# The adaLN weight tiles of a hybrid RWKV-7 and pooling layer: 128 x 512 of one K tile, or four K tiles by 128 columns

## The chip, the cores and the metric

The kernel runs on one NeuronCore of one Trainium2 chip. The metric is device time of one execution, in microseconds (us).

## The reference

One layer of width 2048 (`D`) for 1024 latent tokens and 256 context tokens, in fp32. Only the part that the change touches, and what uses it, matters here:

```
silu_c, silu_cc = silu(c), silu(c_ctx)                   # two vectors of 2048
mod_lat = silu_c @ w_ada + b_ada                         # w_ada: 2048 x 6144
mod_ctx = silu_cc @ w_ada + b_ada
sh, sc, gt = split(mod, 3)                               # shift, scale, gate; 2048 each
h  = rms_norm(x, norm_g) * (1 + sc) + sh                 # latent and context tokens
p  = h @ w_in                                            # 2048 x 6400, combined projection
y  = rwkv7 scan and pooling heads of p, gated
x  = x + gt * (y @ w_out);  return rms_norm(x, final_g)
```

The product of two vectors with `w_ada` reads 50 MB of weights for very little arithmetic.

## The kernel before

Names: PE is TensorE, DVE VectorE, ACT ScalarE, POOL GpSimd, SP SyncE, whose queue issues most DMAs in program order. The kernel is written against a tile framework. Its pools give a tile one of a tag's `bufs` buffers, and a DMA into a buffer waits for the readers of the tile that had it before. The framework orders the instructions of each engine by its own estimate before anything runs; on the chip each engine then goes through its list in that order.

`w_ada` is cut into 12 column blocks `w` of 512 columns (shift 0 to 3, scale 4 to 7, gate 8 to 11) and 16 K tiles `kt` of 128 rows. A weight tile before the change is one K tile by one block, 128 x 512 fp32, 256 KB. The activations `silu` are the stationary operand: 32 columns, of which two are in use (latent and context). The weight tile is the moving operand. `mod_row` (lines 177 to 179) sends K tile `kt` to column group `kt % 4`, that is to PSUM partitions 32 g to 32 g + 31, so that a block gathers four partial sums in four groups of rows. Line 224 (or line 506 for the gate) then multiplies the copied rows with `sel`, which adds the four groups.

The program has four stages in a row:

- Modulation (to about 240 us). `xs`, the tokens, are loaded and squared; `mod(4)` with its tiles in the buffers of `hhi` and `hlo` comes first. Then `mod(5)`, `mod(6)`, `mod(7)`, `mod(0)` to `mod(3)` follow. Beside each stands one `quarter` of two projection tiles: fp16 matmuls of lines 152 to 154, three for each product (`whi` with `hhi`, `whi` with `hlo`, `wlo` with `hhi`), 72 in a quarter, 48 of 512 columns and 24 of 256. `scaled(q)` and `moved(q)` on DVE and ACT make the next `hhi` and `hlo` from the modulation just computed. I call the stretch from one `mod`'s first tiles to the next one's a period. Weight tiles `wa` have a ring of `WAB` = 4 buffers.
- Preparation (to about 970 us): for each of eight j three projection tiles on PE, and beside them the scan's preparation (`prep_kk`, line 379; `prep_scan`, lines 430 and 431 with ACT's tanh, line 437). For j below 4, `gate_row(j)` is issued too, with weight tiles `wg` in a ring of `FB` = 2 buffers.
- The scan with its filler of projections, and the output projection with the residual. Neither reads `w_ada`.

The tiles' DMA and matmul, before:

```
            for kt in range(KT):
                wt = room[kt].bitcast(F32) if room else wap.tile([128, 512], F32, tag="wa", bufs=WAB, name=nm("wa"))
                dma(wt, I["w_ada"][w, kt // 4, :, kt % 4])
                mod_row(kt, wt, ps)
```

Of the kernel before, what the change touches and what calls it, by code (L numbers as in the profile page):

```python
# [7 lines left out]
F32 = mybir.dt.float32  # L8
# [11 lines left out]
KT = 16  # L20
# [25 lines left out]
FB = 2  # L46

WAB = 4
# [10 lines left out]
def hybrid_layer_kernel(ctx: ExitStack, tc: tile.TileContext, I, out, dbg=None):  # L59
    nc = tc.nc  # L60
    mm = nc.tensor.matmul
    V, S, G = nc.vector, nc.scalar, nc.gpsimd
    dma = nc.sync.dma_start
# [8 lines left out]
    def nm(s):  # L72
        cnt[0] += 1
        return f"{s}_{cnt[0]}"

    def bank(tag, bufs=1):
        return psum.tile([128, 512], F32, tag=tag, bufs=bufs, name=nm("ps"))
# [25 lines left out]
    def make_silu(pool):  # L103
        silu = pool.tile([128, KT, 32], F32, name=nm("silu"))
        th0 = pool.tile([128, KT, 2], F32, name=nm("th0"))
        V.memset(silu, 0.0)
        S.activation(th0, cv, AF.Tanh, scale=0.5)
        V.tensor_scalar(th0, th0, 1.0, 0.5, op0=ALU.add, op1=ALU.mult)
        V.tensor_tensor(silu[:, :, 0:2], cv, th0, ALU.mult)
        return silu  # L110
# [18 lines left out]
    wp = ctx.enter_context(tc.tile_pool(name="wp", bufs=1))  # L129
# [44 lines left out]
    idma(sel, I["sel"])  # L174
    silu = make_silu(hc_pool)

    def mod_row(kt, wt, ps):
        g = kt % 4
        mm(ps[32 * g:32 * g + 32, :], silu[:, kt, :], wt, start=(kt < 4), stop=(kt >= 12))


    with ExitStack() as p0:
        xp = p0.enter_context(tc.tile_pool(name="xp", bufs=1))
        wap = p0.enter_context(tc.tile_pool(name="wap", bufs=3))
# [18 lines left out]
        shp = xp.tile([128, KT, 2], F32, name="shp")  # L203
# [10 lines left out]

        def mod(w, room=None):
            ps = bank(("B1", "XU")[w % 2])
            for kt in range(KT):
                wt = room[kt].bitcast(F32) if room else wap.tile([128, 512], F32, tag="wa", bufs=WAB, name=nm("wa"))
                dma(wt, I["w_ada"][w, kt // 4, :, kt % 4])
                mod_row(kt, wt, ps)  # L220
            rows = wp.tile([128, 512], F32, tag="f", bufs=FB, name=nm("rows"))
            S.copy(rows, ps)
            for i in range(4):
                mm(ps[:, 2 * i:2 * i + 2], rows[:, 128 * i:128 * i + 128], sel[:, 0:2], start=True, stop=True)
            V.tensor_tensor(
                modc[:, 4 * w:4 * w + 4, :], ps[:, 0:8].rearrange("p (a b) -> p a b", b=2),
                par[:, PC_BADA + 4 * w:PC_BADA + 4 * w + 4].unsqueeze(2).broadcast_to([128, 4, 2]), ALU.add)
# [15 lines left out]
        def moved(q):  # L243
            V.tensor_scalar(shp[:, 4 * q:4 * q + 4, :], modc[:, 4 * q:4 * q + 4, :], HS, None, op0=ALU.mult)
            for kt, which, xv, rv, hi, lo in segments(q):
                sh = shp[:, kt, which:which + 1]
                S.activation(hi, xv, AF.Identity, bias=sh)
                V.scalar_tensor_tensor(lo, xv, sh, hi, op0=ALU.add, op1=ALU.subtract)

        mod(4, hhi[0:8] + hlo[0:8])  # L250
        for i, (o, n) in enumerate(chunks):
            ps = banks[0][i]
# [6 lines left out]
        for q in range(1, 4):  # L259
            mod(4 + q)  # L260
            quarter(ws, q - 1)
            ws = weights((24, 25), q)
            scaled(q)
        mod(0)
        quarter(ws, 3)
        ws = weights((8, 16), 0)
# [14 lines left out]
        for k in range(2):  # L281
            ps = bank(("B1", "XU")[k])
            for kq in range(4):
                wt = wap.tile([128, 512], F32, tag="wa", bufs=WAB, name=nm("we"))
                dma(wt.rearrange("p (k c) -> p k c", k=4), I["w_in"][24 + k, :, 4 * kq:4 * kq + 4, :])
                for g in range(4):
                    mm(ps[:, 0:2], wt[:, 128 * g:128 * g + 128], shp[:, 4 * kq + g, :],
                       start=(kq + g == 0), stop=(kq + g == 6))
            V.tensor_scalar(eb[:, k, :], ps[:, 0:2], 1.0 / HS, None, op0=ALU.mult)
        quarter(ws, 3)  # L290
# [205 lines left out]

    def gate_row(q):
        ps = bank("B1")
        for kt in range(KT):
            wt = wp.tile([128, 512], F32, tag="f", bufs=FB, name=nm("wg"))  # L500
            dma(wt, I["w_ada"][8 + q, kt // 4, :, kt % 4])
            mod_row(kt, wt, ps)
        rows = wp.tile([128, 512], F32, tag="f", bufs=FB, name=nm("rows"))
        S.copy(rows, ps)
        ps = bank("B1")
        mm(ps[0:32, :], sel[:, 2:34], rows, start=True, stop=True)
        gt = wp.tile([1, 512], F32, tag="f", bufs=FB, name=nm("gt"))
        bg = wp.tile([1, 512], F32, tag="f", bufs=FB, name=nm("bg"))
        dma(bg, I["b_gt"][0:1, 512 * q:512 * q + 512])
        V.tensor_tensor(gt, ps[0:1, :], bg, ALU.add)  # L510
        dma(sGT[0:1, 512 * q:512 * q + 512], gt)
# [18 lines left out]
    for j in range(NP):  # L530
        held = {}
        pre = banks if j == 0 else (None, None)
        kx = hc_pool.tile([128, NALL + 4], F32, tag="k", bufs=2, name=nm("k"))[:, 0:NALL]
        beside(shifted(8 + j, kx, pss=pre[0]))
        drain()
        vx = p1.tile([128, NALL], F32, tag="v", name=nm("v"))
        side.append(prep_kk(j, kx, held))
        beside(shifted(16 + j, vx, pss=pre[1]))
        side.append(prep_v(j, vx))
        rx = p1.tile([128, NTOK], F32, tag="r", name=nm("r"))  # L540
        beside(shifted(j, rx, with_ctx=False, tags=("XU", "B1") if j == 0 else ("d0", "d1")))
        side.append(prep_scan(j, kx, vx, rx, held))
        if j < 4:
            gate_row(j)
# [4 lines left out]
    with ExitStack() as p2s:  # L549
# [368 lines left out]
        for bi, (Q, g) in enumerate(batches):  # L918
            if g == 0:
                carry = {}  # L920
            for s in range(4):
                k = 4 * bi + s
# [121 lines left out]
def layout(x, c, ctx, c_ctx, norm_g, w_ada, b_ada, w_in, shift_mu, w0, w_up, a0, a_up,  # L1044
           k_k, k_a, r_k, lnx_g, lnx_b, w_pool, pool_scale, w_out, final_g):
    import numpy as np

    def cols(a, n):
        return np.asarray(a).reshape(n, 128).T

    L = {}
    L["xT"] = np.asarray(x)[0].T.reshape(KT, 128, NTOK)
    L["ctxT"] = np.asarray(ctx)[0].T.reshape(KT, 128, NCTX)
    L["x"] = np.asarray(x)[0]
    L["cvec"] = np.stack([cols(c, KT), cols(c_ctx, KT)], axis=2)
    L["w_ada"] = np.asarray(w_ada)[0].reshape(4, 4, 128, 12, 512).transpose(3, 0, 2, 1, 4)
    L["w_in"] = np.asarray(w_in)[0].reshape(KT, 128, 50, 128).transpose(2, 1, 0, 3)
    L["w_out"] = np.asarray(w_out)[0].reshape(KT, 128, 4, 512).transpose(2, 0, 1, 3)
    L["w_pool"] = np.asarray(w_pool)[0].reshape(4, 2, 128, 256).transpose(2, 0, 1, 3)
    L["w_up"] = np.asarray(w_up)[0]  # L1060
    L["a_up"] = np.asarray(a_up)[0]
    L["b_gt"] = np.asarray(b_ada)[:, 4096:6144]
    L["final_g"] = np.asarray(final_g)
    L["par"] = np.concatenate([
        cols(norm_g, 16), cols(np.asarray(shift_mu)[0, 0], 26), cols(np.asarray(shift_mu)[0, 1], 26),
        cols(w0, 16), cols(a0, 16), cols(k_k, 8), cols(k_a, 8), cols(r_k, 8), cols(lnx_g, 8), cols(lnx_b, 8),
        cols(pool_scale, 8), cols(b_ada, 48)], axis=1)
    f = np.float32
    L["ident"] = np.eye(128, dtype=f)
    bo = np.zeros((128, 128), f)  # L1070
    bo[:64, :64] = 1
    bo[64:, 64:] = 1
    ex = np.zeros((128, 128), f)
    hs = np.zeros((128, 32), f)
    for h in range(2):
        ex[h::32, 64 * h:64 * h + 64] = 1
        hs[64 * h:64 * h + 64, h] = 1
    L["heads"] = np.concatenate([bo, ex, hs], axis=1)
    r, t = np.arange(128), np.arange(64)[None, :]
    m = np.zeros((128, 2, 2, 128), f)  # L1080
    for h in range(2):
        for d in range(2):
            u = np.where((r // 64 != h) & (d == 1), 63 - r % 64, r % 64)[:, None]
            m[:, h, d, :64] = u < t
            m[:, h, d, 64:] = u <= (63 - t if d else t)
    L["mask"] = m
    rcv = np.zeros((128, 4, 64), f)
    pos = np.arange(64)
    for g, w in enumerate(WINDOWS):
        n = np.clip(pos + w // 2 - 1, 0, 63) - np.clip(pos - w // 2, 0, 63) + 1  # L1090
        rcv[:, g] = (1.0 / n.astype(f)).astype(f)
    L["rc"] = rcv
    se = np.zeros((128, 130), f)
    se[0::32, 0] = 1
    se[1::32, 1] = 1
    se[0::32, 2:] = 1
    L["sel"] = se
    return L
# [18 lines left out]
```

## Time and profile before

| | |
|---|---|
| time, median of 3 runs | 2450.76 us (2447.87 to 2464.92) |
| the profiled execution | 2454.08 us, with a span of 2452.3 us on the engines |
| mean granted TensorE clock | 0.986 |
| busy | PE 2327.6 us (95%), DVE 1639.5 (67%), ACT 786.3 (32%), POOL 389.0 (16%) |
| line 179, `wa` tiles | 224 records (two for each fp32 matmul), 50.8 to 233.5 us |
| line 179, `wg` tiles | 128 records, 286.6 to 620.0 us |
| DMA of `w_ada` | 192 x 256 KB |

A row of the view in order of time gives start in us, length in us, engine, line, operation and `output<-inputs`, with partitions x columns and a count of merged records. The recorded length of a matmul includes its way through the array, so successive rows overlap: what a matmul costs PE is the distance between starts, not the length. A row of the view of stretches gives busy us and, in brackets, the number of instructions of each engine; at its end stand the granted clock, the busy share of the DMA engines and GB/s.

### The profile page before, as it was taken

To read this page: it belongs to the slowest core of one execution; us is meant where nothing else is said; L and a number is where in the kernel's file an instruction comes from. 1 tells how busy PE (TensorE), PEld (TensorE's weight loads), DVE (VectorE), ACT (ScalarE), POOL (GpSimd) and SP (SyncE) were. 2 spreads that over 40 slices of the span, in tenths; PEclk is the share of its full clock that TensorE was granted. 3 is DMA by queue.
4 is the path that set the end of the run, shared out by engine and by line. 5 is a ranking of instruction groups with operands and counts; after the bars stand their busy time and mean duration, and the time that the engine had idled before them with its cause. 6 is when DMAs were issued, how large, how long until landed. Compare 5 with 4: busy or idle time off the path is not lost. (4 is left out here: it accounts for less than half of the span.)

```text
span 2452.3 us, 48416 instructions
## 1 busy us (share of the span) xinstructions
PE 2327.6 (95%) x18702; PEld 1334.8 (54%) x18702; DVE 1639.5 (67%) x3432; ACT 786.3 (32%) x1307; POOL 389.0 (16%) x682
## 2 busy tenths in 40 slices
PE   3999999999999999989998999999999999999997
PEld 0333443534444544445666566656665555788886
DVE  7533664563765666488787977989889784444446
ACT  5233533333444445111122212321232122333334
POOL 3000000100000000113333233333333321000000
PEclk9999999999999999999898999999999999999999
DMA  8666364555543543666556455665565542745546
GB/s 301 183 191 181 100 154 124 141 142 134 131 101 101 126 116 103 177 175 151 149 148 167 131 149 160 164 174 148 158 181 162 141 114 78 236 130 169 183 134 202
DMA packets 421589, 374.45 MB, mean 153 GB/s; under 512 B 232984, under 2 KB 298552, under 8 KB 421104
## 3 DMA queue, kind: packets, MB, share of 16 engines
q1 hardware_dynamic: 403824, 331.75, 48.9%
q0 software_dynamic: 17536, 39.61, 5.7%
q8 instruction: 148, 2.42, 0.4%
q14 instruction: 81, 0.66, 0.1%
HBM read 286.53 MB, written 83.37 MB: 151 GB/s over the span
## 5 line engine op out<-in xcount | busy, mean ns | idle before, releaser
L152 PE MATMUL ps<-hhi,whi 128*128 128x512 f16 x1600 | 611.0, 383 | 2.6 <-ACT whi L144 1.9
L153 PE MATMUL ps<-hlo,whi 128*128 128x512 f16 x1600 | 611.4, 383 | 0.3
L154 PE MATMUL ps<-hhi,wlo 128*128 128x512 f16 x1600 | 610.9, 383 | 0.1
L152 PEld LDWEIGHTS <-whi 128*128 128x128 f16 x1888 | 185.2, 98 | 210.9 <-issue 54.5
L154 PEld LDWEIGHTS <-wlo 128*128 128x128 f16 x1888 | 185.5, 98 | 194.0 <-issue 34.2
L153 PEld LDWEIGHTS <-whi 128*128 128x128 f16 x1888 | 185.7, 98 | 186.7 <-issue 35.3
L145 DVE SCALAR_TENSOR_TENSOR wlo<-wraw,whi 128x512 f16<-128x512 f32 x200 | 136.0, 683 | 131.9 <-ACT whi L144 131.2
L144 ACT ACTIVATE whi<-wraw 128x512 f16<-128x512 f32 x200 | 124.2, 629 | 308.3 <-PE ps L153 198.6
L696 DVE TENSOR_TENSOR tm<-TT 64x30 f32<-64x30 f32 (+2 forms) x600 | 195.5, 326 | 18.0 <-DMA TT<-dn 9.1
L698 DVE TENSOR_TENSOR TT<-TT,tm 64x30 f32<-64x30 f32 (+2 forms) x600 | 197.7, 330 | 8.5
L975 PE MATMUL ps<-wolo,mhi 128*128 128x512 f32 x512 | 199.7, 390 | 2.2 <-DVE wolo L971 2.1
L975 PE MATMUL ps<-wohi,mlo 128*128 128x512 f32 x512 | 198.9, 389 | 0.0
L975 PE MATMUL ps<-wohi,mhi 128*128 128x512 f32 x512 | 198.2, 390 | 0.4 <-ACT wohi L970 0.4
L971 DVE TENSOR_TENSOR wolo<-wo,wohi 128x512 fp32r<-128x512 f32 x144 | 97.9, 689 | 147.1 <-ACT wohi L970 146.8
L970 ACT CAST wohi<-wo 128x512 fp32r<-128x512 f32 x144 | 89.2, 621 | 176.9 <-PE ps L975 151.4
L664 PE MATMUL ps<-AR,BK 64*128 64x128 f32 (+1 forms) x1280 | 122.6, 296 | 17.8 <-DMA BK<-sBK 8.7
L664 PEld LDWEIGHTS ps<-AR,BK 64*128 64x128 f32 x1280 | 105.4, 198 | 46.2 <-issue 13.4
L744 POOL DMA_DIRECT2D SUV<-sV x160 | 96.6, 607 | 128.5 <-PE ps L805 65.1
L975 PEld LDWEIGHTS ps<-wolo,mhi 128*128 128x128 f32 x512 | 96.1, 188 | 24.0 <-DVE wolo L971 4.1
L975 PEld LDWEIGHTS ps<-wohi,mhi 128*128 128x128 f32 x512 | 95.9, 188 | 21.8 <-ACT wohi L970 2.0
L975 PEld LDWEIGHTS ps<-wohi,mlo 128*128 128x128 f32 x512 | 96.1, 188 | 19.7
L813 POOL TENSOR_TENSOR S<-St,PCt 128x256 f32<-128x256 f32 x76 | 57.5, 757 | 262.5 <-DVE St L807 231.1
(226 smaller groups left out, 3450.8 us busy)
## 6 DMA issues: line engine op xcount, KB each, us to landing
wraw<-in_w_in SPq DMA_DIRECT2D x200, 256.0 KB
BK<-sBK SPq DMA_DIRECT2D x156, 256.0 KB
wo<-in_w_out SPq DMA_DIRECT2D x144, 256.0 KB
wa<-in_w_ada SPq DMA_DIRECT2D x112, 256.0 KB
wg<-in_w_ada SPq DMA_DIRECT2D x64, 256.0 KB
AR<-sAR SPq DMA_DIRECT2D x64, 256.0 KB
sBK<-BK SPq DMA_DIRECT2D x32, 320.0 KB
sBK<-BK SPq DMA_DIRECT2D x16, 640.0 KB
```

The source lines that it names most:

```text
L144: S.activation(whi, raw, AF.Copy, scale=WS)
L145: V.scalar_tensor_tensor(wlo, raw, WS, whi, op0=ALU.mult, op1=ALU.subtract)
L152: mm(ps[:, :n], w[0][:, k, :], hi[kt][:, o:o + n], start=(kt == 0), stop=False)
L153: mm(ps[:, :n], w[0][:, k, :], lo[kt][:, o:o + n], start=False, stop=False)
L154: mm(ps[:, :n], w[1][:, k, :], hi[kt][:, o:o + n], start=False, stop=(kt == KT - 1))
L664: mm(ps[h][:, 64 * ns * u:64 * ns * (u + 1)], BK[hs, p, d, :], AR[hs, :, p, d, :], start=True, stop=True)
L696: V.tensor_tensor(tm, TT[:, 0:s, s:s + 1].broadcast_to([64, s, n]), TT[:, s:s + 1, s + 1:32].broadcast_to([64, s, n]), ALU.mult)
L698: V.tensor_tensor(TT[:, 0:s, s + 1:32], TT[:, 0:s, s + 1:32], tm, ALU.add)
L744: (idma if d else dma)(SUV[hss[1 - h], h, :, d, :], sV[Q, cn, h])
L970: S.copy(whi, raw)
L971: V.tensor_tensor(wlo, raw, whi.bitcast(F32), ALU.subtract)
L975: mm(banks[q, t], mix[k][m][:, tk], w, start=(k == order[0] and n == 0), stop=(k == order[-1] and n == 2))
```

## The change

A weight tile is now four K tiles by 128 columns: `[128, 4, 128]`, again 2 KB for each of 128 partitions. The host lays `w_ada` out so that a tile is one piece of memory. Tile `i` of a block holds column piece `c = i // 4` and K tiles `4 a` to `4 a + 3` with `a = i % 4`. Its four matmuls, of 128 columns each, go to the four column groups; before, one matmul of 512 columns went to one group. Number and size of DMAs, the sums, the buffers and everything behind the rows in PSUM stay. The last lines of the diff's middle part (`we`) only rename a shape.

```
-    def mod_row(kt, wt, ps):
-        g = kt % 4
-        mm(ps[32 * g:32 * g + 32, :], silu[:, kt, :], wt, start=(kt < 4), stop=(kt >= 12))
+    def mod_block(i, wt, ps):
+        c, a = i // 4, i % 4
+        for g in range(4):
+            mm(ps[32 * g:32 * g + 32, 128 * c:128 * c + 128], silu[:, 4 * a + g, :], wt[:, g],
+               start=(a == 0), stop=(a == 3))
...
-            for kt in range(KT):
-                wt = room[kt].bitcast(F32) if room else wap.tile([128, 512], F32, tag="wa", bufs=WAB, name=nm("wa"))
-                dma(wt, I["w_ada"][w, kt // 4, :, kt % 4])
-                mod_row(kt, wt, ps)
+            for i in range(16):
+                if room:
+                    wt = room[i].bitcast(F32).rearrange("p (g n) -> p g n", g=4)
+                else:
+                    wt = wap.tile([128, 4, 128], F32, tag="wa", bufs=WAB, name=nm("wa"))
+                dma(wt, I["w_ada"][w, i])
+                mod_block(i, wt, ps)
...
-                wt = wap.tile([128, 512], F32, tag="wa", bufs=WAB, name=nm("we"))
-                dma(wt.rearrange("p (k c) -> p k c", k=4), I["w_in"][24 + k, :, 4 * kq:4 * kq + 4, :])
+                wt = wap.tile([128, 4, 128], F32, tag="wa", bufs=WAB, name=nm("we"))
+                dma(wt, I["w_in"][24 + k, :, 4 * kq:4 * kq + 4, :])
...
-        for kt in range(KT):
-            wt = wp.tile([128, 512], F32, tag="f", bufs=FB, name=nm("wg"))
-            dma(wt, I["w_ada"][8 + q, kt // 4, :, kt % 4])
-            mod_row(kt, wt, ps)
+        for i in range(16):
+            wt = wp.tile([128, 4, 128], F32, tag="f", bufs=FB, name=nm("wg"))
+            dma(wt, I["w_ada"][8 + q, i])
+            mod_block(i, wt, ps)
...
-    L["w_ada"] = np.asarray(w_ada)[0].reshape(4, 4, 128, 12, 512).transpose(3, 0, 2, 1, 4)
+    L["w_ada"] = np.asarray(w_ada)[0].reshape(4, 4, 128, 12, 4, 128).transpose(3, 4, 0, 2, 1, 5).reshape(12, 16, 128, 4, 128)
```

The line of the adaLN matmul is 179 before and 181 after. The order of PE's list, too, comes out differently. In the modulation stage, in the period of `mod(6)`, PE's list before reads (names are tiles with their running number; `32x512` is 32 rows out by 512 columns):

```order
L179 MATMUL ps_594<-wa_619,silu_179 32x512
L179 MATMUL ps_594<-wa_622,silu_179 32x512
L154 LDWEIGHTS wlo_560
L154 MATMUL ps_334<-hhi_112,wlo_560 128x512
L152 LDWEIGHTS whi_559
L152 MATMUL ps_334<-hhi_113,whi_559 128x512
L153 LDWEIGHTS whi_559
L153 MATMUL ps_334<-hlo_129,whi_559 128x512
L179 MATMUL ps_594<-wa_625,silu_179 32x512
```

After the change, a stretch of the same period, where `x4` counts the matmuls of one tile:

```order
L181 MATMUL ps_690<-wa_721,silu_179 32x128 x4
L152 LDWEIGHTS whi_655
L152 MATMUL ps_334<-hhi_112,whi_655 128x512
L154 LDWEIGHTS wlo_656
L154 MATMUL ps_334<-hhi_111,wlo_656 128x512
L181 MATMUL ps_690<-wa_727,silu_179 32x128 x4
L152 LDWEIGHTS whi_655
L152 MATMUL ps_335<-hhi_112,whi_655 128x512
L152 LDWEIGHTS whi_655
L152 MATMUL ps_336<-chi_145,whi_655 128x256
```

Where one or two tiles stood between groups of three or more fp16 matmuls, one tile now stands between groups of two or three. A period still begins with four tiles in a row.

In the preparation stage, beside `prep_scan` of j = 1, PE's list before and then after reads:

```order
L153 MATMUL ps_2790<-hlo_125,whi_2794 128x512
L179 MATMUL ps_2726<-wg_2763,silu_179 32x512
L179 MATMUL ps_2726<-wg_2766,silu_179 32x512
L154 LDWEIGHTS wlo_2795
L154 MATMUL ps_2790<-hhi_109,wlo_2795 128x512
L152 LDWEIGHTS whi_2812
L152 MATMUL ps_2790<-hhi_110,whi_2812 128x512
```

```order
L437 MATMUL ps_3326<-lora_2080,ulo_3318 128x512
L181 MATMUL ps_3158<-wg_3207,silu_179 32x128 x4
L154 LDWEIGHTS wlo_3337
L154 MATMUL ps_3269<-hhi_116,wlo_3337 128x512
L152 LDWEIGHTS whi_3336
L152 MATMUL ps_3269<-hhi_117,whi_3336 128x512
L181 MATMUL ps_3158<-wg_3213,silu_179 32x128 x4
L436 LDWEIGHTS uhi_3317
L436 MATMUL ps_3330<-lora_2080,uhi_3317 128x512
```

A pair of gate tiles that stood together is now parted by two fp16 matmuls.

More of the change, by code (lines that the diff above doesn't have):

```diff
@@ L283, in hybrid_layer_kernel @@
             for kq in range(4):
-                wt = wap.tile([128, 512], F32, tag="wa", bufs=WAB, name=nm("we"))
-                dma(wt.rearrange("p (k c) -> p k c", k=4), I["w_in"][24 + k, :, 4 * kq:4 * kq + 4, :])
+                wt = wap.tile([128, 4, 128], F32, tag="wa", bufs=WAB, name=nm("we"))
+                dma(wt, I["w_in"][24 + k, :, 4 * kq:4 * kq + 4, :])
                 for g in range(4):
-                    mm(ps[:, 0:2], wt[:, 128 * g:128 * g + 128], shp[:, 4 * kq + g, :],
+                    mm(ps[:, 0:2], wt[:, g], shp[:, 4 * kq + g, :],
                        start=(kq + g == 0), stop=(kq + g == 6))
```

## The prediction

> **What bounds the kernel now.** I read the page first, then the stretches of the program, then single instructions in order of time.
>
> ```profile
> span 2452.3 us, 48416 instructions
> PE 2327.6 (95%) x18702; PEld 1334.8 (54%) x18702; DVE 1639.5 (67%) x3432; ACT 786.3 (32%) x1307; POOL 389.0 (16%) x682
> PE   3999999999999999989998999999999999999997
> PEclk9999999999999999999898999999999999999999
> ```
>
> PE is busy in every slice after the first, at full clock. So PE's time is what a change has to shorten, and it has to do so where PE itself is late and not where it waits. The adaLN matmuls stand in slices 1 to 11 only (40 to 620 us). The next view cuts the modulation stage into one period per `mod`, first for all instructions, then for line 179 (`mod_row`) alone.
>
> ```profile
> core 0: us, PE busy (x) PEld busy (x) DVE busy (x) ACT busy (x) POOL busy (x), PEclk, DMA share, GB/s
> 106.59:133.12 26.53, 26.01 (x113) 8.57 (x113) 14.38 (x23) 7.62 (x13) 0.00 (x0) 1.00 0.65 189
> 185.79:212.38 26.59, 25.95 (x114) 8.57 (x113) 8.18 (x13) 7.59 (x12) 0.16 (x3) 1.00 0.61 178
> ...
> 106.59:133.12 26.53, 11.53 (x32) 1.54 (x33) 1.00 0.65 189
> ```
>
> A period is 26.5 us, 11.5 of them line 179, while DVE, ACT and the DMA engines (0.65 of their time) have room. What line 179 costs PE is read from its neighbours (start, length, instruction):
>
> ```profile
> 59.31 0.38 PE L154 MATMUL ps<-hhi,wlo 128*128 128x512 f16 x1
> 59.52 0.38 PE L152 MATMUL ps<-hhi,whi 128*128 128x512 f16 x1
> 59.83 1.04 PE L179 MATMUL ps<-wa,silu 128*32 128x512 f32 x2
> 60.81 0.39 PE L153 MATMUL ps<-hlo,whi 128*128 128x512 f16 x1
> ...
> 106.38 0.27 PE L154 MATMUL ps<-chi,wlo 128*128 128x256 f16 x1
> 106.59 1.07 PE L179 MATMUL ps<-wa,silu 128*32 128x512 f32 x8
> 107.58 0.60 PE L152 MATMUL ps<-hhi,whi 128*128 128x512 f16 x2
> ```
>
> A plain fp16 matmul of 512 columns follows the one before after 0.21 us (59.31 to 59.52), one of 256 after half of it. One adaLN matmul (two records: fp32 goes in two passes) puts 59.52 to 60.81 = 1.29 us where 0.22 stood: it costs 1.07. Four of them, on four column groups, put 106.38 to 107.58 = 1.20 where 0.11 stood: 1.09. So a **run** of one to four matmuls of kernel before costs the same 1.07 us: the groups do work at once, but most runs use one or two. Counted in the order of PE, the 176 matmuls that stand between others (7 `mod` and 4 gates) make 120 runs: 71 in `mod`, 49 in the gates. 120 x 1.07 = 128 us.
>
> **What a run costs after the change.** No run of before has 128 columns on four groups. The nearest row is `prep_kk`'s line 379: also fp32, also 32 weight columns on each of four groups, other moving data for each, 320 columns.
>
> ```profile
> 272.07 0.38 PE L154 MATMUL ps<-hhi,wlo 128*128 128x512 f16 x1
> 272.38 0.75 PE L379 MATMUL ps<-sqk,heads 128*32 128x320 f32 x8
> 273.06 0.39 PE L152 MATMUL ps<-hhi,whi 128*128 128x512 f16 x1
> ```
>
> 0.99 us where 0.22 stood: 0.775. From 512 columns (1.09) to 320 (0.775) that is 1.64 ns a column, so 128 columns give 0.775 - 192 x 1.64 ns = **0.46 us** (my estimate; two passes of 0.105 and 0.25 for entering, leaving and the second pass's weights). A tile that directly follows a tile adds its two passes only. A weight load takes 108 ns, no less than a pass of 128 columns, so I put 0.22:
>
> ```profile
> L179 PEld LDWEIGHTS ps<-wa,silu 128*32 128x32 f32 x224 | 10.9, 108 | 34.2 <-issue 21.7 <-DMA wa<-in_w_ada 11.7 <-PE ps L153 0.8
> ```
>
> The tiles now make 151 runs: 92 of the 112 in `mod` (after four back to back, each tile stands alone) and 59 of the 64 in the gates. `mod`: 92 x 0.46 + 20 x 0.22 = 46.7 against 71 x 1.07 = 76.0, a gain of 29.3. Gates: 59 x 0.46 + 5 x 0.22 = 28.2 against 49 x 1.07 = 52.4, a gain of 24.2. **PE is given back 53.5 us.** `mod(4)`, the first, has 4, 2 and 10 tiles in a row in both orders and its groups are full already; I count it at 0.
>
> **What comes late next.** Its tiles. SP's queue waits for PE to free a buffer, and then PE for the landing:
>
> ```profile
> SPq L219 <- PE ps L179: 104.1, 69, 5.5
> ...
>   issue: 41.2, 103
>   DMA wg<-in_w_ada: 17.9, 23
>   DMA wa<-in_w_ada: 13.4, 20
> ...
> 107.66 0.33 SPq L219 DMA_DIRECT2D wa<-in_w_ada  x1
> ...
> 110.24 0.38 PE L154 MATMUL ps<-hhi,wlo 128*128 128x512 f16 x1
> 110.77 2.19 PE L179 MATMUL ps<-wa,silu 128*32 128x512 f32 x4
> 112.89 0.39 PE L153 MATMUL ps<-hlo,whi 128*128 128x512 f16 x1
> ```
>
> The four tiles at 106.59 give their buffers back together; SP issues the next from 107.66. PE takes the first at 110.77, 3.1 us after its issue and 0.2 later than PE was ready (entering takes 0.31), and can have the second at 112.89 - 0.98 = 111.9 only: 1.36 us of waiting in the period. Bounds for a tile's way from issue to use: 3.1 and about 4.2; I take 3.5, since the later tiles of a period are issued singly. With the run (0.36) and the way to SP (0.1) a buffer comes round in 4.0 us; four buffers (`WAB`) give a tile each 1.0 us. The new order asks for one each 0.95: behind the four tiles and 1.73 us of fp16 work, eleven gaps hold 5.4 us of fp16 work, 0.49 each, plus 0.46. So 11 x 0.05 = 0.6 us of new waiting in a period: 7 x 0.6 = **4 us back**. What stands behind the waiting matmul is all of PE's queue.
>
> The gates have two buffers (`FB`), so a tile each 4.0 / 2 = 2.0 us. Waits of 17.9 us for 4 gates show it already; one of them:
>
> ```profile
> 501.44 0.38 PE L431 MATMUL ps<-lora,ulo 128*128 128x512 f16 x1
> 501.75 2.23 PE L179 MATMUL ps<-wg,silu 128*32 128x512 f32 x4
> 503.91 0.39 PE L430 MATMUL ps<-lora,uhi 128*128 128x512 f16 x1
> ```
>
> A pair that should leave after 0.98 us leaves after 2.16. In the new order of the second gate 13.0 us of dense fp16 work, 2.2 us of lines 430 and 431 and twelve runs of 0.46 stand behind its first four tiles: 1.72 us for each of 12 tiles, less than two buffers give, and unevenly (every second gap is 0.2 to 0.6 us). That is 12 x 0.28 = 3.4 us of waiting from the mean alone and about as much from unevenness, against 17.9 / 4 = 4.5 before. Bounds: 0 and 5 us more per gate; I take 2, **8 us back**.
>
> The DMAs keep 2 KB for each partition (128 rows of 512 floats, now four pieces of 128 columns that lie side by side), so their time stays. SP's, DVE's and ACT's instructions are the same apart from places exchanged in these stages; from shortly behind the last gate to the end every engine's order is as before, so the two later stages only start earlier. DVE's 14.38 us of work in a period still fit into 23. The cover is thin in the first period alone, where the first `scaled` has to keep pace with PE; a rival below prices that.
>
> **Sum** against the profiled execution (2454.1, with a span of 2452.3): 2454.1 - 53.5 + 4 + 8 = 2412.6. The median of the runs, 2450.8, lies 3.3 lower: **2410** (2409.3 rounded up).
>
> **Rivals.**
>
> *Waits do not grow* (0.20). If a single tile comes in 3.1 us, four buffers give one each 0.9 and neither ring binds: 2454.1 - 53.5 = 2400.6, and up to 5 less if the waits after the four tiles fall, so 2392 to 2397 by the median. For it: the 3.1. Against: the 1.1 us that the second tile lagged.
>
> *The rings bind* (0.17). With 4.2 us from issue to use a buffer takes 4.66: 1.17 a tile in `mod`, 0.22 x 11 = 2.4 a period, 17 in all; 2.33 in the gates, 12 x 0.61 = 7.3 and 2 for unevenness against 4.5, 5 each and 20 in all: 2454.1 - 53.5 + 37 = 2437.6, or 2434 by the median; where half the tiles take so long, 2422. Then SP waits less for PE, and PE for the landing.
>
> *Other engines come late* (0.13). Where no gate stands beside the scan's preparation, PE waits for ACT's tanh:
>
> ```profile
> PE ps L430 <- ACT th L437: 8.6, 4, 2.8
> ```
>
> That is 2.2 us for each of the last four j, and nearly nothing while gates fill the gap. If it comes back in the four gate j, 9 us, and 3 in the first period: 2412.6 + 12, or 2421 by the median.
>
> *The second pass's loads are not hidden* (0.04). A load of 108 ns behind each first pass makes a run 0.57: 151 x 0.11 = 17 more, 2426. The row of the eight loads of line 379 speaks against it:
>
> ```profile
> 272.38 0.16 PEld L379 LDWEIGHTS ps<-sqk,heads 128*32 128x32 f32 x8 [0.42 <-issue]
> ```
>
> All eight lie in the first 0.16 us, beside matmuls whose first pass lasts 0.29. The Trainium skill, "TensorE: Matmul & The Clock Gate", section "Part 3: Packing small matmuls", says that weight loads overlap matmuls in flight only where the row group differs. Here all four share the rows, so by that rule this rival would hold; the trace does not agree.
>
> *The four run one after another* (0.03), the case that ends slower. If at 128 columns the groups did not overlap, a tile is 8 passes of 0.107 and 0.25 around them, 1.1 us: 151 x 1.1 + 25 x 0.86 = 188 against 128, +59, 2513. It turns to a loss once a run costs over (128 - 25 x 0.22) / 151 = 0.81 us. Against it: the 1.07 us that four of 512 columns take here.
>
> **How the numbers follow.** Forecast 0.43, rivals 0.20, 0.17, 0.13, 0.04 and 0.03. A measurement of this kernel tells about 1% (24.5 us, 2426) from no change. Faster by over 1%: 0.43 + 0.20 + 0.13 + half of 0.17 and of 0.04 = 0.86; within: 0.11; slower: 0.03. Range: from the waits that shrink (2392, and one for rounding) to past the loads' case (2426) and into the rings that bind (2422 to 2434): 2391 to 2430; beyond it lie a third of the rings' chance and the slower case.
>
> **What would show it.** In the profile after: line 181's tiles alone should stand 0.67 to 0.69 us from the fp16 matmul before to the one behind (now 1.29); a `mod` period 23.0 us (now 26.5: 10 x 1.07 less 13 x 0.46 and 3 x 0.22, and 0.6 of waiting); the gate stretch about 4 us shorter each; waits of line 181 for `wa` up by some 4 us and for `wg` by some 8; the time from the last gate to the end as before, 1830 us. The forecast is wrong if a run is not near 0.46, or if waits for tiles eat more than 25 us.

## The result, and the profile after

The kernel after takes 2387.79 us (median of 4 runs, 2384.81 to 2398.54) against 2449.32 for the kernel before (4 runs beside it): a ratio of 0.9746, 95% interval 0.9711 to 0.978. A later set with more runs gives 0.9764 (0.9735 to 0.9794). It is faster, as forecast, but by more: 61.5 us in the first comparison where 41 were forecast, and 2387.8 lies 3 us under the range. All 15 runs of it in this study together have a median of 2391.6 us.

The head of the page, after:

```profile
span 2387.4 us, 50718 instructions
PE 2252.8 (94%) x19854; PEld 1342.6 (56%) x19854; DVE 1637.4 (69%) x3432; ACT 785.7 (33%) x1307; POOL 380.2 (16%) x682
```

PE has 1152 instructions more (each tile eight records for two) and 75 us less to do. It still bounds the kernel: it is busy in 94% of a shorter span.

In the view of stretches, one period of the modulation, first all instructions, then line 181 alone:

```profile
98.15:119.66 21.51, 20.80 (x209) 9.48 (x209) 13.88 (x21) 7.13 (x12) 0.00 (x0) 1.00 0.69 221
141.38:164.50 23.12, 20.83 (x209) 9.49 (x208) 8.17 (x14) 8.71 (x16) 0.00 (x0) 1.00 0.65 206
...
98.15:119.66 21.51, 6.19 (x128) 2.70 (x129) 1.00 0.69 221
```

The period fell from 26.5 to between 21.5 and 23.1 us (forecast 23.0; the five periods after the first, from 75.40 to 186.75 us, have a mean of 22.3), and line 181 takes 6.19 of it where line 179 took 11.53. Instruction by instruction, a tile alone and four in a row:

```profile
122.55 0.38 PE L153 MATMUL ps<-hlo,whi 128*128 128x512 f16 x1
122.86 0.42 PE L181 MATMUL ps<-wa,silu 128*32 128x128 f32 x8
123.22 0.39 PE L154 MATMUL ps<-hhi,wlo 128*128 128x512 f16 x1
...
119.46 0.27 PE L154 MATMUL ps<-chi,wlo 128*128 128x256 f16 x1
119.66 1.08 PE L181 MATMUL ps<-wa,silu 128*32 128x128 f32 x32
120.67 0.39 PE L152 MATMUL ps<-hhi,whi 128*128 128x512 f16 x1
```

From the fp16 matmul before to the one behind it is 123.22 - 122.55 = 0.67 us where 1.29 stood, so a run costs 0.67 - 0.21 = 0.46: exactly the estimate. Four in a row cost 120.67 - 119.46 - 0.11 = 1.10, or 0.22 for each further tile (0.46 + 3 x 0.22 = 1.12).

The stages, worked out from the starts of the same instructions in four profiles of each kernel (first sum of `mod(4)`, last sum of `mod(3)`, first matmul of `prep_kk` for each j, first and last matmul of the scan's step, end), in us:

| stage | before (4 profiles) | after (4 profiles) | forecast change |
|---|---|---|---|
| modulation, to `prep_kk` of j = 0 | 272.4, 269.6, 270.2, 272.2 | 243.3, 243.7, 253.5, 243.8 | -25.3 |
| j = 0 to 4, with the four gates | 391.2, 389.3, 390.7, 389.4 | 366.6, 366.2, 365.4, 366.5 | -16.2 |
| j = 4 to 7 | 261.8, 261.6, 262.1, 261.6 | 261.2, 262.1, 262.4, 261.2 | 0 |
| to the first step of the scan | 171.0, 173.2, 171.4, 168.7 | 171.5, 172.2, 171.5, 171.4 | 0 |
| scan | 947.9, 944.3, 937.7, 942.2 | 936.9, 938.9, 933.4, 937.3 | 0 |
| to the end | 408.0, 408.5, 408.2, 409.8 | 407.9, 408.0, 409.3, 407.9 | 0 |

So three terms are to be explained: the modulation (27.5 without the one profile of 253.5), the gates (24.0 where 16.2 were forecast), and the scan, whose list of instructions did not change and which was 11.0 us shorter in the first pair of profiles.

### The profile page after: what moved, and what is told of

It reads as the page before. It is cut to its first block, busy times and chain, and to the rows that moved or that the text cites. A ratio compares the mean times of both kernels' runs of the same rounds, so it can differ in the third digit from the quotient of the medians.

```text
span 2387.4 us, 50718 instructions
## 1 busy us (share of the span) xinstructions
PE 2252.8 (94%) x19854; PEld 1342.6 (56%) x19854; DVE 1637.4 (69%) x3432; ACT 785.7 (33%) x1307; POOL 380.2 (16%) x682
## 5 line engine op out<-in xcount | busy, mean ns | idle before, releaser
L144 ACT ACTIVATE whi<-wraw 128x512 f16<-128x512 f32 x200 | 123.1, 628 | 262.4 <-PE ps L153 196.3
L670 PEld LDWEIGHTS ps<-AR,BK 64*128 64x128 f32 x1280 | 104.5, 196 | 44.7 <-issue 14.6
```

Of the source, the lines that this page charges most:

```text
L144: S.activation(whi, raw, AF.Copy, scale=WS)
L670: mm(ps[h][:, 64 * ns * u:64 * ns * (u + 1)], BK[hs, p, d, :], AR[hs, :, p, d, :], start=True, stop=True)
```

## Experiments

**The two kernels again, and each half of the change alone.** The first two are unchanged. Each half takes its part of `w_ada` in its own layout. The number behind "Measured" is the time as a share of the kernel before's, with its 95% interval.

Kernel before again: 

> The kernel before, unchanged, as a second profile. Theory A (the scan stage is 11.0 us shorter in the profile after only because one execution differs from another): its scan stage, from the first to the last matmul of line 781, falls anywhere between 936 and 948 us. Theory B (the change shortens it, although no instruction there stands in another place): again 947 to 949 us. Both: ratio 1.00, modulation and gates as in the first profile within 1 us (first tile behind the first period to the last gate tile 540 us).

Measured: 0.9999 (0.998 to 1.0018); scan stage 944.3 us. The modulation takes 2.8 us less than in the first profile and the gates 1.9 less, more than the 1 us that was expected; in the modulation the clock stood at half for 6.8 us there and for nothing here.

Kernel after again: 

> The kernel after, unchanged, as a second profile. Theory A: scan stage anywhere between 936 and 948 us. Theory B: 936 to 938 us again. Both: 54 us less than before up to the end of the preparation stage, ratio 0.975.

Measured: 0.9781 (0.9762 to 0.9801); scan stage 938.9 us; modulation and gates as in its first profile within 0.5 us.

New tiles in `mod` only:

```
...
-        for i in range(16):
-            wt = wp.tile([128, 4, 128], F32, tag="f", bufs=FB, name=nm("wg"))
-            dma(wt, I["w_ada"][8 + q, i])
-            mod_block(i, wt, ps)
+        for kt in range(KT):
+            wt = wp.tile([128, 512], F32, tag="f", bufs=FB, name=nm("wg"))
+            dma(wt, I["w_adb"][q, kt // 4, :, kt % 4])
+            mod_row(kt, wt, ps)
...
```

> New tiles in the eight mod blocks, old tiles in the four gates. If the stages add up: 29 us less by the first matmul of line 379, nothing from the gates, so 29 us in all (ratio 0.988), plus what the scan stage does. Theory A: no part of the scan's 11 us belongs to it more than to any other run. Theory B: the scan stage is shorter here or in the next kernel by some 5 to 11 us. A rival that the gates' gain is only work moved from the modulation (tiles and matmuls shifted across the border): the gates would take 2 us more or less than in the kernel before.

Measured: 0.9882 (0.9859 to 0.9904), 29.6 us. The gates take 388.6 us, 1.6 less than the mean of the kernel before: next to nothing moved across the border. But the modulation takes 251.8 us in this profile, 19 less than the mean of before and not 29. The clock stood at half for 30.7 us of it, as in the third profile of the kernel after below (253.5 us), against 10.2 us in the other profiles of the kernel after; 20.5 us more at half clock are worth up to 10.2. Its scan stage takes 940.2 us.

New tiles in the gates only, the same edit in `mod`: 

> New tiles in the four gates, old tiles in the mod blocks. If the stages add up: the modulation as before, 6.3 us less for each gate, 25 us in all (ratio 0.990). The prediction's theory that the ring of two buffers eats 2 us of each gate: 16 us (0.9935).

Measured: 0.9926 (0.9904 to 0.9949), 20.7 us by the medians. Its stages tell more: modulation 270.6 us as before, gates 365.7 us, 24.5 less than the mean of before, 6.1 for each gate. That is as much as PE was given back (24.2); what the ring has to do with it is read below. Its scan stage takes 942.9 us. The two halves add up to the whole within the intervals (29.6 + 20.7 = 50.3 and 53.5).

**Is it the four groups?**

```
-            mm(ps[32 * g:32 * g + 32, 128 * c:128 * c + 128], silu[:, 4 * a + g, :], wt[:, g],
-               start=(a == 0), stop=(a == 3))
+            mm(ps[32 * a:32 * a + 32, 128 * c:128 * c + 128], silu[:, 4 * a + g, :], wt[:, g],
+               start=(g == 0), stop=(g == 3))
```

> The tile stays four K tiles by 128 columns with four matmuls, but all four go to one column group (the tile's number a), so that they add up one after another; sums, DMAs and number of matmuls stay. Theory of the document (what the change gains is that the four groups work at once): a tile takes eight passes of 0.107 us and 0.25 around them, 1.1 us, and 0.86 where it follows a tile; 126 runs and 50 further tiles: 182 us against 75, so some 107 us slower than the kernel after and 50 slower than before (ratio 1.02). Rival (the gain is that pieces of 128 columns or one contiguous DMA are cheaper in themselves): within 1% of the kernel after. Scan stage: 936 to 939 us if the change's number of instructions shortens it, 944 to 948 if only the change's timing does, anywhere between if chance does.

Measured: 1.0011 (0.9994 to 1.0027). The whole gain is gone, so it comes from the groups and neither from the pieces nor from the contiguous DMA. But it is not the loss of 50 us that was expected. In the order of time of this kernel, a tile alone and two in a row:

```profile
63.28 0.38 PE L152 MATMUL ps<-hhi,whi 128*128 128x512 f16 x1
63.59 1.06 PE L181 MATMUL ps<-wa,silu 128*32 128x128 f32 x8
64.58 0.39 PE L153 MATMUL ps<-hlo,whi 128*128 128x512 f16 x1
...
56.48 0.27 PE L154 MATMUL ps<-chi,wlo 128*128 128x256 f16 x1
56.69 1.53 PE L181 MATMUL ps<-wa,silu 128*32 128x128 f32 x16
58.32 0.38 PE L152 MATMUL ps<-hhi,whi 128*128 128x512 f16 x1
```

One tile costs 64.58 - 63.28 - 0.21 = 1.09, as expected. But two cost at most 58.32 - 56.48 - 0.11 = 1.73, and 1.55 in most of this kernel's runs of two, not 1.96: the second tile has another group, and its first matmul starts at 57.15, before the last of the first tile at 57.47. And the longer runs take the place of the waits for tiles, of which this kernel has almost none (PE and its tiles, up to 240 us):

```profile
PE ps L181 <- DMA wa<-in_w_ada: 0.4, 1, 0.4
```

The modulation takes 282.0 us against 269.6 to 272.4 before, the gates 387.6 against 389.3 to 391.2. The scan stage takes 935.3 us, under both of the narrow ranges expected, which leaves chance.

**The rings.** Three kernels change one number each: `WAB` = 5, `WAB` = 3, `FB` = 3.

```
-WAB = 4
+WAB = 5
```

> The kernel after with five buffers for the mod tiles in place of four. If PE's waits for these tiles (1.65 us in a period, 11 in all by the profile after) come from the ring: 5 to 10 us less than the kernel after, the waits near 0.5 a period. If the DMA's rate sets them: the same as the kernel after within 3 us.

Measured: 0.9758 (0.9716 to 0.98), the same as the kernel after. Waits for `wa` as PE shows them, in the kernel after and with five buffers:

```profile
PE ps L181 <- DMA wa<-in_w_ada: 10.5, 18, 1.5
```

```profile
PE ps L181 <- DMA wa<-in_w_ada: 8.4, 14, 1.7
```

The modulation loses 2.8 us of its 243.3 (240.5), and this view shows 2.1 us less of waiting: less than the 5 to 10 expected.

> The kernel after with three buffers for the mod tiles. With the prediction's 3.5 us from issue to use (a buffer comes round in 4.0) a tile comes each 1.33 us against 1.22 that the order asks for here: waits of 2.5 us in a period against 1.65, some 6 us slower than the kernel after. With 2.8 us, as the gates' tiles of the profile after suggest (3.29 us from a tile to the next but one without a wait): no more waits than now, within 3 us of the kernel after.

Measured: 0.9765 (0.9733 to 0.9797), the same again.

```profile
PE ps L181 <- DMA wa<-in_w_ada: 9.3, 20, 1.4
```

Not one more us of waiting with three buffers, as the shorter way from issue to use (2.8 us) has it and not the prediction's 3.5. The framework's order put the tiles farther apart here (100 runs instead of 92). Up to the last `mod` this kernel took 6.9 us more (163.1 against 156.2), and 4.3 less from there to `prep_kk` (35.7 against 40.0). Up to 3.4 of these 4.3 are the clock's, which stood at half there for 6.8 us in the kernel after and for nothing here. What the 6.9 are made of was not taken apart.

> The kernel after with three buffers for the gate tiles in place of two. The prediction's theory (two buffers hold the gates back by some 6 us each): the gates take 4 us less each, 16 us less than the kernel after in all. What the profile after says (waits of 1.4 us for each gate): at most 1.4 us less each, 4 to 6 us in all.

Measured: 0.9744 (0.9715 to 0.9772). The gates take 364.0 us, 2.2 less than the mean of the kernel after, where the ring of two as the prediction priced it would have given back some 16. The waits for `wg` and for ACT's tanh, from 240 to 662 us, in the kernel after and with three buffers:

```profile
PE ps L436 <- ACT th L443: 5.1, 6, 2.8
PE ps L181 <- DMA wg<-in_w_ada: 4.1, 10, 1.1
```

```profile
PE ps L436 <- ACT th L443: 9.8, 7, 2.8
PE ps L181 <- DMA wg<-in_w_ada: 2.7, 6, 0.7
```

This view counts only time in which no matmul is recorded. By the starts of the matmuls (worked out below), the tiles' waits fall from 5.5 to 7.0 us to some 2 to 4, while PE waits longer for the tanh: 7.0 us instead of 2.1 up to the first `prep_kk` of j = 4, where the rest of both rows lies. So two buffers cost the four gates some 4 us in all and not 16, and ACT takes back part of what a third one gives.

Both `FB` = 3 and the other two are the kernel after within their intervals; none is a better version that could be told from it.

**The scan.** Two more profiles of each kernel.

> A third profile of the kernel before, for the scan stage alone (first to last matmul of line 781; so far 947.9 and 944.3 us before, 936.9 and 938.9 after). Theory A, chance: anywhere from 935 to 948. Theory B, the change shortens it: 944 to 948.

Measured: 2442.1 us, scan stage 937.7 us: in the kernel before, as short as in the kernel after.

> A third profile of the kernel after, and its ratio with a narrow interval. Stages up to the last line 379: 871 to 872 us, as in its two profiles. Theory A: scan stage anywhere from 935 to 948, ratio near 0.9785 (51.5 us, what the stages up to the scan give). Theory B: scan 936 to 939, ratio near 0.975.

Measured: 0.9764 (0.9735 to 0.9794); scan stage 933.4 us, but the stages up to the last `prep_kk` take 881.4, 10 us more than expected, all of it in the modulation (253.5).

> A fourth profile of the kernel before, for the scan stage. Theory A, chance: anywhere from 935 to 948 us. Theory B: 944 to 948.

Measured: 2445.77 us, scan stage 942.2 us.

> A fourth profile of the kernel after, for the scan stage. Theory A, chance: anywhere from 935 to 948 us. Theory B: 936 to 939.

Measured: 2389.92 us, scan stage 937.3 us.

One thing that differs from profile to profile is the granted clock. Two views of stretches at the same steps of the scan, in the first profile of the kernel before and in the third:

```profile
1320.00:1335.00 15.00, 12.64 (x221) 8.26 (x221) 5.42 (x11) 4.56 (x8) 2.52 (x4) 0.77 0.62 151
1400.00:1410.00 10.00, 7.58 (x67) 5.44 (x67) 6.24 (x17) 1.64 (x3) 2.31 (x4) 0.83 0.56 183
```

```profile
1318.00:1333.00 15.00, 14.41 (x298) 10.26 (x298) 10.85 (x30) 5.88 (x11) 2.90 (x5) 1.00 0.58 151
1398.00:1408.00 10.00, 9.81 (x114) 5.41 (x112) 9.53 (x28) 1.91 (x4) 2.79 (x5) 1.00 0.61 174
```

The last column but two is the clock: 0.77 and 0.83 against 1.00, and PE gets through 221 and 67 matmuls instead of 298 and 114. The clock falls to 0.50 in pieces of 3.4 us or whole multiples of it. Added up over the scan from the records of the clock, half clock held for 37.5, 27.3, 20.5 and 30.7 us in the four profiles of before and for 23.9, 27.3, 23.9 and 23.9 in those of after; the four scans of before in the order of these sums are 937.7, 944.3, 942.2 and 947.9 us long. A stretch at half clock costs at most half its length, so 37.5 against 23.9 can explain up to 6.8 of the 11.0 us by which the first two profiles differ. Theory B as written (944 to 948 for the kernel before) falls with 937.7. Whether a few us remain is open: the means of the scan differ by 6.4 us, their half clock by 4.2 us, which is worth at most 2.1. The changed kernels leave it open too: their scans are 940.2 us (new tiles in `mod` only), 942.9 (in the gates only), 935.3 (one group), 941.2 (`WAB` = 5), 939.1 (`WAB` = 3) and 938.9 (`FB` = 3). The one-group kernel, as slow as the kernel before in all, has one of the shortest scans; `WAB` = 5, as fast as the kernel after, has 941.2 with only 20.5 us at half clock. So the clock is not all of the spread either.

The clock does explain the 253.5. In that profile PE ran 17 us in one piece at half clock behind the column sums of the edge (the fp32 matmuls of two columns, line 293 after), where the profile with `FB` = 3 ran at full clock at the same place:

```profile
217.00:234.00 17.00, 17.00 (x62) 11.06 (x61) 3.25 (x7) 4.93 (x8) 0.00 (x0) 0.50 0.25 75
```

```profile
205.00:222.00 17.00, 17.00 (x123) 12.67 (x122) 9.11 (x15) 10.94 (x16) 0.27 (x2) 1.00 0.59 187
```

62 matmuls against 123 in the same time. Over the whole modulation the clock stood at half for 30.7 us in that profile and for 10.2 in each of the three others of the kernel after. The 20.5 us between them are worth up to 10.2, and 253.5 is 9.9 above the others' mean.

## Why the prediction was right and wrong

*PE is the bound, and a run's price.* Right. 0.46 us for a run and 0.22 for a further tile were measured as worked out from line 379, and a period gave back what they say: 26.4 us before and 22.3 after in the mean of five, 4.2 less, against 10 x 1.07 - 13 x 0.46 - 3 x 0.22 = 4.1 from the prices alone. That matmuls of 128 columns would not overlap, or that weight loads would show, is refuted by the same rows: a run with loads that wait would have cost 0.57. So the Trainium skill's rule ("TensorE: Matmul & The Clock Gate", section "Part 3: Packing small matmuls") that a load overlaps only where the row group differs, beside which the same section names loads into a background weight buffer, does not hold as it stands for four column groups on the same rows here: 0.46.

*Waits in `mod`.* The sum is right, its place is luck. To measure waits for tiles in both kernels alike, take the distance between the fp16 matmuls on both sides of a run, and subtract the first one's own 0.21 (or 0.11) and the run's price (1.07 before; 0.46 and 0.22 for each further tile after). What is left over the seven `mod` is 11.2 to 12.4 us in the four profiles before and 14.6 to 15.8 in those after, some 3.5 more; 4 were forecast. But the forecast spread them as 0.6 over every period, and in the six later periods the waits did not grow: 1.6 to 1.7 us a period before, 1.4 to 1.7 after. They grew in the first, from about 2 us to between 5 and 7.5, which the sum put at nothing. The modulation gave 27.5 us where 25.3 were forecast, although the clock stood at half for longer after (10.2 us, and 30.7 in one profile, against 0 to 6.8).

*Waits in the gates.* This step failed, in its sign. The prediction gave back 8 us there, since a buffer was to come round in 4.0 us, two buffers so to give a tile each 2.0, and the order to ask for one each 1.72. Measured in the same way, the waits for gate tiles were 14.0 to 15.3 us before and 5.5 to 7.0 after: 8 less, not 8 more. (The 17.9 us before that the prediction read include idle time of the weight loads; PE's own row of that wait has 3.3 and the loads' 14.7, and PE's hides what the second tile of a pair waits.) The prices (24.2) and these 8 make 32, but the gates gave only 24.0 us, because other waits in the same stretch grew by some 7 to 8. The main rows of the view of waits from 240 to 662 us, before and then after:

```profile
PE ps L430 <- ACT th L437: 0.4, 2, 0.2
```

```profile
PE ps L436 <- ACT th L443: 5.1, 6, 2.8
PE ps L512 <- ACT rows L510: 3.5, 2, 1.9
PE ps L154 <- DVE wlo L145: 1.3, 2, 0.7
```

Line 512 is the gate's product with `sel`, which waits for ACT's copy of the rows: 2.6 to 3.5 us in the four profiles, and no such row before. Of the 5.1 for the tanh 2.1 lie before j = 4 begins at 609.9 us (1.4 to 2.4 in the four profiles); the rest belongs to j = 4, where no gate stands and the kernel before waits 2.8 too. So that the gates gave just what PE was given back comes of two changes that cancel: the tiles came in time where the sum had them late, and ACT and DVE came late where the sum had nothing.

Why the tiles came in time, the last gate of the kernel after shows:

```profile
555.82 0.42 PE L181 MATMUL ps<-wg,silu 128*32 128x128 f32 x8
...
556.72 0.43 PE L181 MATMUL ps<-wg,silu 128*32 128x128 f32 x8
...
559.12 0.43 PE L181 MATMUL ps<-wg,silu 128*32 128x128 f32 x8
559.48 0.39 PE L437 MATMUL ps<-lora,ulo 128*128 128x512 f16 x1
559.71 0.38 PE L152 MATMUL ps<-hhi,whi 128*128 128x512 f16 x1
560.01 0.43 PE L181 MATMUL ps<-wg,silu 128*32 128x128 f32 x8
```

A tile follows the next but one after 3.30 us (555.82 to 559.12) and 3.29 (556.72 to 560.01), and PE does not wait: 559.71 to 560.01 is the bare 0.30 of entering. So a buffer comes round in 3.3 us or less, and issue to use takes at most 3.3 - 0.36 - 0.1 = 2.8 us. The prediction's bounds, 3.1 and 4.2, were read where four tiles had been issued in a row. The 4.2 counts from the first tile's issue at 107.66; the second's own was at 108.08, so it took 3.8. And 3.1 is no lower bound for tiles issued one at a time, which these are. Nor is 2.8 an upper one: the page of the kernel after has a median of 3.1 from issue to landing, of the landings that its trace tells (22 of 64, from 2.6 to 5.1).

```profile
wg<-in_w_ada SPq DMA_DIRECT2D x64, 256.0 KB, 3.1
```

With 3.3, two buffers give a tile each 1.65, and the order's 1.72 fits. That a shorter round trip is all of the 8 us is not shown: the new order also parted the pairs, whose second tile waited before, and no run here tells whether a tile that is one piece of memory lands sooner. The rival "waits do not grow", at a chance of 0.20, comes nearest: it held for the tiles of the gates and of the six later periods.

*The scan at nothing.* The price was right for its list of instructions, but the profile that the sum started from was one whose scan had more half clock than any other of the study (37.5 us). The prediction's own row of the clock has an 8 in slices 20 and 22, both in the scan, where the text read full clock throughout. Against the means of four profiles the change gives 27.5 + 24.0 = 51.5 us where 41.5 were forecast, nearly 8 of the difference in the gates, and the scan's 6.4 beside it stand open by some 4. A range taken from single profiles has to allow for that, and this one did not.

*The other rivals.* "Other engines come late" (12 us in all, 9 of them from the tanh in the gates) came true in part, under the gates' gain: 1 to 2 us from the tanh, some 3 from the rows' copy. `mod(4)`, counted at 0, gave 1.0 us on average (to its sum 48.2 us against 49.2), within the spread of the profiles.

## What to carry to other kernels

In this kernel a matmul with 32 weight columns on one column group cost PE as much time (1.07 us) as four on four groups (1.09), so cut the moving operand so that whatever arrives together fills all groups; what it gives is read from the distances between the neighbours' starts, and from a row with the same shape of groups and another number of columns. A round trip of a buffer has to be read where the loads are issued as they will be: here the last gate's tiles, issued singly, were there at most 2.8 us after their issue, the first two of four in a burst after at most 3.1 and 3.8. A stage that gains what was worked out may do so by two changes that cancel: add up the waits for every engine in it, between the same two instructions in both kernels. And before a few us are explained, add up the clock in the stage, in more than one profile.

## What was not expected of the hardware

TensorE's granted clock halves in pieces of 3.4 us while the profile shows PE busy throughout: behind the two-column fp32 matmuls it stayed at 0.50 for nothing, 3.4, 6.8 or 20.5 us in executions of kernels with the same instructions there. In the four profiles of the kernel after it was 3.4, 3.4, 6.8 and 20.5 us, and from the last `mod`'s sum to the first `prep_kk` took 38.3, 38.4, 40.0 and 46.6 us. Why the length of the piece differs, no run here shows. The Trainium skill ("TensorE: Matmul & The Clock Gate", section "Part 1: The HAM clock gate") tells of a gate of half or full clock with a free-running window of 3.4 us; pieces of 3.4 us at 0.50 agree with it.
